# A hybrid-attention layer on one core: row copies moved from engines to DMA, weights loaded one step sooner, two head-stage steps issued later

## The chip, the core and the metric

The kernel runs on one core of a Trainium2 chip. The metric is the device time of one execution in microseconds (us). Of the program of before, three timed executions are shown, and one execution was profiled.

## What is computed

One layer on x of 1024 rows (the sequence) by 1024 columns, in float32 accuracy:

- h = RMSNorm(x) and P = h @ W_in. P's columns are split between two kinds of attention, which run beside each other.
- **mla**: 8 heads with compressed queries and keys, 96 numbers per head (64 plain, 32 rotated), 64 values, a block-causal mask over chunks of 64 rows, softmax.
- **ca**: 8 heads of 64 numbers; each chunk of 64 rows attends to itself and the 8 chunks before it, with a learned bias per head that depends on the clipped distance, softmax.
- x += concat(RMSNorm(mla), RMSNorm(ca)) @ W_out, and x += W_down(silu(g) * u), where [g|u] is a causal convolution of width 3 over RMSNorm(x) @ W_up.

## The kernel before, in words

TensorE (PE) multiplies in float32r, so every operand is held as a high and a low part and a product takes three matmuls (`mm3`, lines 136 to 139). The program order of every engine's queue is written out by hand; the tile framework adds only the waits (for data, and for a buffer that is to be used again). An instruction that waits holds up all that stands behind it in its own queue, and that goes for SyncE's queue (SP) of DMA issues and for GpSimd's (POOL) too.

The stages, by the span of the profiled execution: the latent projection (to about 75 us), 32 steps of the projection for the ca heads (to about 230), 16 heads (231 to 510), the output projection (to about 620), and the feed-forward layer.

**The 32 steps** (loop at line 818). Step i multiplies with one block of weights: `load_wc` (523) issues its DMA on SP, two steps ahead (819, 820); `split_wc` (547) makes its high part on ScalarE (ACT, 552) and its low part on VectorE (DVE, 553) one step ahead. Stages, weights and their parts all take buffers of one ring of ten (`p2`, 111), of which two more are taken for good at step 22 by `new_bias`. From step 22 on, `run_slot` puts the preparation of heads 0 and 1 between the matmuls.

**Preparation of a head** (`prep`, 652): a list of small jobs with a due time m. For head n from 2 on, m counts steps of the head stage from two heads earlier; for the first two heads it is mapped to the slots of the 32 steps. The jobs: `tr` transposes q and k on PE; `q_hi`, `k_hi` write their high parts (ACT, 674 and 682) and `q_lo`, `k_lo` the low ones (DVE, 678 and 688) into the operand set of the head (QH, K1, K2, QL, 1024 columns each; three sets in turn). A ca head has only 64 rows, so high and low parts are stacked: `dup_q` (690) and `dup_k` (696) copy 64 rows of 4 KB each, by DMAs that POOL issues; `zero` (693) clears 32 rows of QL on POOL. `bias_load` (711) fetches the bias table on SP. `mx` (732) computes the scores' maxima for the softmax on PE in 11 jobs, for ca with all 128 stacked rows, which DVE reduces in `mx_post` (739: lines 745, 749, 750); `mmax`, `mr` (756) and `mr_post` (758) turn the maxima into one row, which a DMA issued by POOL (760) puts into QL. Mask rows: `set_rows` (609) writes rows 96 to 112 of K2 and QL on ACT with two instructions (612), once for each of the three sets; `zero_rows` (605) clears 32 rows of K2 (607), on POOL for set 0 and on DVE for set 2, the latter at step 4 of the head stage (`ZERO_AT`, 962).

**The head stage** (loop at line 1110): 12 steps per head, even heads ca, odd heads mla. Step s computes scores of one tile (`score`, 901: matmuls 908 to 922, exponentials on ACT, 927 to 935); a step later `split` (938) makes the low part of the exponentials (948 to 950), on DVE for the steps of a head that `PLO_V` names, else on POOL; three steps later `pv` (953) multiplies with the values (958 to 960). After a head's last tile `finish` (1007) stores the 1024 sums by DMA (1011), and at step +3 `rec` (1013) inverts them, stores them to DRAM (1016) and loads them back spread over 64 rows (1017); ten and eleven steps later `mul` (1019) scales the output. For each pair of heads `o_sq` (967) squares on ACT (978) and adds to the running sums of squares on DVE, for one pair on POOL (979).

## Time and profile before

| | us |
|---|---|
| median of 3 timed executions | 1270.3 |
| lowest, highest of them | 1268.56, 1270.39 |
| the profiled execution's own time | 1271.62 |
| its span, first to last instruction | 1269.9 |
| PE busy | 1221.0 |
| DVE busy | 940.8 |
| POOL busy | 704.6 |
| ACT busy | 648.8 |

How to read it: the span is what the rows of the trace add up to; the profiled execution's own time is 1.72 us longer, and 1.3 us above the median. Busy times are sums over the span, and matmuls overlap one another in part. A row of the timeline names the start, the length, the engine, the source line, the operation, output and inputs, and in brackets the time that the engine stood idle before it and what ended that.

### The profile page before, as it was taken

What the parts mean: (1) busy time and instruction counts of PE and PEld (TensorE: products, weight loads), DVE (VectorE), ACT (ScalarE), POOL (GpSimd) and SP (SyncE); (2) the same over time, 40 slices, a digit from 0 to 9 for tenths busy, and PEclk for the clock granted to TensorE, in tenths of its full rate; (3) what the DMA queues carried; (4) which work ended last, traced back from release to release, by engine and by line L of the source; (5) the groups of instructions that cost most, each with busy time, mean ns of one, the idle gap of its engine ahead of it and who ended that gap; (6) DMA issues with size and microseconds to landing.
All of it is one profiled execution on the core that took longest, in us unless ns stands there. A gap on an engine that the chain in (4) does not pass through costs nothing.

```text
span 1269.9 us, 17774 instructions
## 1 busy us (share of the span) xinstructions
PE 1221.0 (96%) x5888; PEld 1004.7 (79%) x5888; DVE 940.8 (74%) x1623; ACT 648.8 (51%) x1338; POOL 704.6 (55%) x710
## 2 busy tenths in 40 slices
PE   9999998899998998999889999999999999999998
PEld 9888876787786876788668888888888888878887
DVE  6678565688888895466898766767776677888983
ACT  7562254678877887405555434334334344434442
POOL 4689750466564668204488767667677640425630
PEclk9999998999999999999999999999999999999999
DMA  9111213111111221265413332333322256933153
GB/s 353 36 35 50 59 56 78 26 44 43 27 37 37 43 64 52 100 232 174 141 59 121 120 99 84 108 108 105 119 81 86 91 181 243 363 92 116 59 197 127
DMA packets 102637, 134.78 MB, mean 106 GB/s; under 512 B 12152, under 2 KB 60816, under 8 KB 102544
## 3 DMA queue, kind: packets, MB, share of 16 engines
q1 hardware_dynamic: 100752, 129.37, 31.3%
q0 software_dynamic: 1792, 4.26, 1.7%
q8 instruction: 47, 0.77, 0.3%
q14 instruction: 46, 0.38, 0.1%
HBM read 97.47 MB, written 31.81 MB: 102 GB/s over the span
## 4 chain that ended last, share of the span: by engine, by line
PE 50%; DVE 8%; issue 2%; ACT 1%; POOL 1%; DVEq 0%; POOLq 0%; ACTq 0%
PE pb L139 11%; PE pb L138 11%; PE pb L137 11%; PE ps L137 6%; PE ps L139 5%; PE ps L138 5%; DVE ps L1438 1%; DVE as L1422 1%; DVE hq L1242 1%; POOL plo L950 1%; DVE wop L1359 1%; DVE h L1206 0%; DVE as L1421 0%; DVE as L1423 0%; DVE as L1424 0%
## 5 line engine op out<-in xcount | busy, mean ns | idle before, releaser
L950 POOL TENSOR_TENSOR plo<-misc,phi 128x512 fp32r<-128x512 f32 (+3 forms) x116 | 119.1, 1029 | 58.0 <-ACT phi L935 42.7
L1383 ACT ACTIVATE u<-ps,cols 128x1024 f32<-128x1024 f32 x44 | 53.2, 1208 | 178.0 <-DVE ps L1438 178.0
L137 PE MATMUL ps<-hq,wop 128*128 128x512 f32 x344 | 135.0, 393 | 2.6 <-ACT wop L1354 1.5
L139 PE MATMUL ps<-hq,wop 128*128 128x512 f32 x344 | 134.2, 390 | 1.8 <-DVE wop L1359 1.8
L138 PE MATMUL ps<-hq,wop 128*128 128x512 f32 x344 | 134.0, 390 | 0.2 <-DVE hq L1242 0.2
L138 PE MATMUL pb<-wring,aring 128*128 128x512 f32 x308 | 120.7, 392 | 2.1 <-DVE wring L1613 2.1
L137 PE MATMUL pb<-wring,aring 128*128 128x512 f32 x308 | 120.6, 391 | 0.3 <-DVE x2b L1438 0.3
L139 PE MATMUL pb<-wring,aring 128*128 128x512 f32 x308 | 120.6, 391 | 0.0
L1359 POOL TENSOR_TENSOR wop<-S,wop 128x512 fp32r<-128x512 f32 x42 | 63.3, 1507 | 96.4 <-ACT wop L1354 96.4
L137 PE MATMUL pb<-hq,wop 128*128 128x512 f32 x264 | 103.0, 390 | 2.3 <-ACT wop L1354 2.2
L139 PE MATMUL pb<-hq,wop 128*128 128x512 f32 x264 | 103.1, 390 | 0.2 <-DVE wop L1359 0.2
L138 PE MATMUL pb<-hq,wop 128*128 128x512 f32 x264 | 102.7, 389 | 0.0
L1610 DVE TENSOR_TENSOR aring<-ast,aring 128x512 fp32r<-128x512 f32 x77 | 71.1, 924 | 37.6 <-ACT aring L1609 37.6
L1609 ACT ACTIVATE aring<-ast 128x512 fp32r<-128x512 f32 x77 | 48.5, 630 | 93.7 <-PE pb L138 74.0
L932 ACT ACTIVATE misc<-pb 128x512 f32<-128x512 f32 (+3 forms) x116 | 56.3, 485 | 47.9 <-PE pb L918 20.0
L137 PEld LDWEIGHTS ps<-hq,wop 128*128 128x128 f32 x344 | 64.5, 188 | 20.0 <-DVE ps L1438 4.9
L138 PE MATMUL pb<-wl,hTh 128*128 128x512 f32 x192 | 75.8, 395 | 2.0 <-DVE wl L553 1.9
L139 PEld LDWEIGHTS ps<-hq,wop 128*128 128x128 f32 x344 | 64.6, 188 | 16.0 <-DVE wop L1359 2.5
L137 PE MATMUL pb<-wh,hTh 128*128 128x512 f32 x192 | 76.2, 397 | 0.0
L139 PE MATMUL pb<-wh,hTl 128*128 128x512 f32 x192 | 75.6, 394 | 0.0
L138 PEld LDWEIGHTS ps<-hq,wop 128*128 128x128 f32 x344 | 64.6, 188 | 13.7 <-DVE hq L1242 0.6
L204 POOL TENSOR_TENSOR stat<-stat,mhalf 128x1 f32<-128x1 f32 (+2 forms) x50 | 72.7, 1454 | 4.2
(331 smaller groups left out, 3629.8 us busy)
## 6 DMA issues: line engine op xcount, KB each, us to landing
wstage<-in_w_up_dram SPq DMA_DIRECT2D x43, 512.0 KB, 4.2
ast<-act_scratch SPq DMA_DIRECT2D x77, 256.0 KB, 4.5
act_scratch<-as SPq DMA_DIRECT2D x44, 256.0 KB, 2.3
wd<-in_w_down_dram SPq DMA_DIRECT2D x44, 256.0 KB, 5.5
act_scratch<-u SPq DMA_DIRECT2D x33, 256.0 KB, 2.1
x<-in_x_dram SPq DMA_DIRECT2D x16, 512.0 KB, 7.2
ws<-in_w_in_dram SPq DMA_DIRECT2D x32, 256.0 KB, 2.6
x_scratch<-x SPq DMA_DIRECT2D x14, 512.0 KB, 3.0
```

The lines of the kernel that those rows point to most:

```text
L137: T.matmul(o, lh, rh, start=start, stop=False)
L138: T.matmul(o, lh, rl, start=False, stop=False)
L139: T.matmul(o, ll, rh, start=False, stop=stop)
L204: G.tensor_tensor(dst, dst, mhalf[:, :n], op=ALU.pow)
L932: A.activation(p32[:, w], o[:, w], AF.Exp, scale=sc_)
L950: e.tensor_tensor(plo[:, w], p32[:, w], f(phi[:, w]), op=ALU.subtract)
L1242: lo_eng.tensor_tensor(lo, s3[:, ks], f(hi), op=ALU.subtract)
L1359: (V if n in W_LO_V or (j, n) in W0_LO_V else G).tensor_tensor(lo, s, f(hi), op=ALU.subtract)
L1383: A.activation(u, U, AF.Identity, scale=convw(2, c), bias=convb(c))
L1422: V.tensor_tensor(s[1], s[0], A11, op=ALU.subtract)
L1609: A.activation(ah, s, AF.Copy)
L1610: V.tensor_tensor(al, s, f(ah), op=ALU.subtract)
```

## The change

- `set_rows` writes the mask rows once, for set 0, on POOL instead of ACT, at slot 9; `copy_rows` copies them, for ca together with the zeroed rows of K2, to sets 1 and 2 by DMAs on SP. `zero_rows` clears its rows for set 0 alone, on POOL, and stores a block of zeros to DRAM; `zero` then loads QL's 32 rows of zeros from there (not for head 0, where `zero_rows` has cleared them).
- `dup_q`, `dup_k` and the DMA of `mr_post` are issued by SP instead of POOL.
- `mx` of head 0 uses the 64 rows of the high parts alone, and not the stacked 128.
- From step 20 of the 32 on, weights are loaded three steps ahead.
- In mla heads `PLO_V` no longer names step 6, so POOL makes that low part.
- `o_sq`'s additions for the second and third pair come three steps later than the squares; `spread`, the load of the inverted sums, comes two steps after `rec` (heads 0 to 13).

```diff
--- before.py
+++ after.py
@@ -31,8 +31,9 @@
 PI_IN = 3.1415925
 PHI_M = 24
 PHI_0 = 18
-PLO_V = (1, 3, 6, 8, 10)
+PLO_V = (1, 3, 6, 8, 10), (1, 3, 8, 10)
 LAG = 3
+WC_AHEAD = 20
 MR = 18
 MX_CA = 9
 STORE = 2
@@ -49,7 +50,6 @@
 OSQ_G = ("mla", 2),
 SIDE_AT = 3
 SIDE_2 = 5, 6, 8
-ZERO_AT = 4
 WARM = 18
 END_PLO_V = range(180, 192, 2)
 
@@ -554,6 +554,7 @@
             wsp[i] = wh, wlo
 
     dsc = nc.dram_tensor("bias_scratch", (2, 8, 384), F32, kind="Internal").ap()
+    dzero = nc.dram_tensor("zero_scratch", (32, 1024), F32, kind="Internal").ap()
     dden = nc.dram_tensor("den_scratch", (16, 1024), F32, kind="Internal").ap()
     mcols = [const([128, 24], F32, f"mcol{i}") for i in range(2)]
     mrow = const([8, 128], F32R, "mrow")
@@ -602,15 +603,24 @@
         st = sets[i]
         st.QH, st.K1, st.K2, st.QL = [b[:, 1024 * i:1024 * i + 1024] for i in range(4)]
 
-    def zero_rows(i):
-        if heads[i][0] == "ca":
-            (V if i == 2 else G).memset(f(sets[i].K2[64:96]), 0.0)
-
-    def set_rows(i):
-        st = sets[i]
+    def zero_rows():
+
+        st = sets[0]
+        G.memset(f(st.K2[64:96]), 0.0)
+        G.memset(f(st.QL[64:96]), 0.0)
+        nc.sync.dma_start(dzero, f(st.QL[64:96]))
+
+    def set_rows():
+        st = sets[0]
         for dst, c in ((st.K2, 0), (st.QL, 16)):
-            A.activation(dst[96:113].rearrange("p (t i) -> p t i", t=16),
-                         mk[96:113, c:c + 16, None].to_broadcast([17, 16, 64]), AF.Copy)
+            G.tensor_copy(dst[96:113].rearrange("p (t i) -> p t i", t=16),
+                          mk[96:113, c:c + 16, None].to_broadcast([17, 16, 64]))
+
+    def copy_rows(i):
+
+        r = 64 if heads[i][0] == "ca" else 96
+        nc.sync.dma_start(f(sets[i].K2[r:113]), f(sets[0].K2[r:113]))
+        nc.sync.dma_start(f(sets[i].QL[97:113]), f(sets[0].QL[97:113]))
 
     def new_v(i):
         b = sv(F32R, "vset")
@@ -688,13 +698,13 @@
             V.tensor_tensor(o, p[0:d], f(st.K2[0:d, c]), op=ALU.subtract)
 
         def dup_q():
-            G.dma_start(st.QH[64:128], st.QH[0:64])
+            nc.sync.dma_start(f(st.QH[64:128]), f(st.QH[0:64]))
 
         def zero():
-            G.memset(f(st.QL[64:96]), 0.0)
+            nc.sync.dma_start(f(st.QL[64:96]), dzero)
 
         def dup_k():
-            G.dma_start(st.K1[0:64], st.K2[0:64])
+            nc.sync.dma_start(f(st.K1[0:64]), f(st.K2[0:64]))
 
         def v_post():
             if n < 2:
@@ -733,7 +743,7 @@
             p = hold["m", j] = bank()
             for t, part, k_, w, off in jobs()[j]:
                 w = max(w, 256)
-                q_, k2 = (st.QH, st.K1) if is_ca else (st.QH[0:d], st.K2[0:d])
+                q_, k2 = (st.QH, st.K1) if is_ca and n else (st.QH[0:d], st.K2[0:d])
                 T.matmul(p[:, off:off + w], q_[:, t * 128:t * 128 + 128], k2[:, k_:k_ + w], start=True, stop=True)
 
         def mx_post(j):
@@ -757,7 +767,7 @@
 
         def mr_post():
             V.tensor_scalar(mrow, hold.pop(("m", 10))[0:8, 0:128], -1.0, None, op0=ALU.mult)
-            G.dma_start(st.QL[96:97].rearrange("p (t s) -> p t s", t=8), mrow)
+            nc.sync.dma_start(f(st.QL[96:97]).rearrange("p (t s) -> p t s", t=8), f(mrow))
 
         r = [(1, "pe", lambda: tr(0, 0)), (2, "pe", lambda: tr(0, 1)), (3, "pe", lambda: tr(1, 0)),
              (4, "pe", lambda: tr(1, 1)),
@@ -765,7 +775,9 @@
              (4, "post", lambda: k_hi(0)), (4, "post", lambda: q_lo(1)),
              (5, "post", lambda: k_hi(1)), (5, "post", lambda: k_lo(0)), (6, "post", lambda: k_lo(1))]
         if is_ca:
-            r += [(1, "post", zero), (4, "post", dup_q), (5, "post", dup_k), (-1, "post", lambda: bias_load(0)), (6, "post", bias_nat),
+            if n:
+                r += [(1, "post", zero)]
+            r += [(4, "post", dup_q), (5, "post", dup_k), (-1, "post", lambda: bias_load(0)), (6, "post", bias_nat),
                   (6, "post", lambda: bias_load(1)), (14, "post", bias_tr)]
         for j in range(11):
             m = min((MX_CA if is_ca else 6) + max(j - 1, 0), 17)
@@ -816,8 +828,10 @@
                 fn()
 
     for i, (c, k, ts) in enumerate(steps):
-        if i + 2 < len(steps):
+        if i == WC_AHEAD:
             load_wc(i + 2)
+        if i + 2 + (i >= WC_AHEAD) < len(steps):
+            load_wc(i + 2 + (i >= WC_AHEAD))
         if i < 4:
             rope_tables(i)
         if i == 3:
@@ -847,12 +861,12 @@
                         first.setdefault((b, ph), []).append(fn)
                     else:
                         micro.setdefault((first_slot(n, m, ph), n, m, PH.index(ph)), []).append(fn)
-            micro[16, 9, 0, 0] = [lambda: set_rows(0)]
-            micro[26, 9, 0, 0] = [lambda: set_rows(1)]
+            micro[9, 9, 0, 0] = [set_rows]
+            micro[20, 9, 0, 0] = [lambda: copy_rows(1)]
         if i == 24:
             for n in range(2):
                 new_set(n)
-                zero_rows(n)
+            zero_rows()
         for t in ts:
             if i >= 22:
                 run_slot(slot)
@@ -889,14 +903,14 @@
     OB = [misc[:, 1024 * i:1024 * i + 1024] for i in range(2)]
     bias_tab(misc[:, 2048:2944])
     new_set(2)
-    set_rows(2)
+    copy_rows(2)
     opair, O, wo, sqs = {}, {}, {}, {}
 
     turn = [0]
 
     def plo_v(s, n):
 
-        return s % 12 in PLO_V if n < 14 else s in END_PLO_V
+        return s % 12 in PLO_V[n % 2] if n < 14 else s in END_PLO_V
 
     def score(s, n, i, pc_):
         kind, h = heads[n]
@@ -959,24 +973,32 @@
         T.matmul(o[0:64], vs.VL[:, kt, :], phi[:, 0:n], start=False, stop=False)
         T.matmul(o[0:66], vs.VH[:, kt, :], plo[:, 0:n], start=False, stop=stop)
 
-    later = {ZERO_AT: [lambda: zero_rows(2)]}
+    later = {}
 
     def at(s, fn):
         later.setdefault(s, []).append(fn)
 
-    def o_sq(kind, j, c):
+    def o_sq(kind, j, c, s0):
+
         w = slice(c, c + 512)
         o = opair[kind, j][:, w]
         if j == 0:
             if c == 0:
                 sqs[kind] = blk(F32, "sqs")
             A.activation(sqs[kind][:, w], o, AF.Square)
+            return
+        if c == 0:
+            opair["sq"] = blk(F32, "sq")
+        sq = opair["sq"][:, w]
+        A.activation(sq, o, AF.Square)
+
+        def add():
+            (G if (kind, j) in OSQ_G else V).tensor_tensor(sqs[kind][:, w], sqs[kind][:, w], sq, op=ALU.add)
+
+        if j < 3:
+            at(s0 + 3, add)
         else:
-            if c == 0:
-                opair["sq"] = blk(F32, "sq")
-            sq = opair["sq"][:, w]
-            A.activation(sq, o, AF.Square)
-            (G if (kind, j) in OSQ_G else V).tensor_tensor(sqs[kind][:, w], sqs[kind][:, w], sq, op=ALU.add)
+            add()
 
     def o_part(kind, j, c):
 
@@ -1012,9 +1034,10 @@
 
         def rec():
             V.reciprocal(d8, d8)
-            row = dden[n]
-            nc.sync.dma_start(row.rearrange("(p c) -> p c", c=8), d8)
-            nc.sync.dma_start(R[64:128], dap(row, 0, [[0, 64], [1, 1024]]))
+            nc.sync.dma_start(dden[n].rearrange("(p c) -> p c", c=8), d8)
+
+        def spread():
+            nc.sync.dma_start(R[64:128], dap(dden[n], 0, [[0, 64], [1, 1024]]))
 
         def mul(c):
             if (kind, h // 2) not in opair:
@@ -1024,13 +1047,14 @@
                             op=ALU.mult)
 
         at(s + 3, rec)
+        at(s + (5 if n < 14 else 3), spread)
         s0 = s + (11 if n < 14 else 9)
         at(s0 - 1, lambda: mul(0))
         at(s0, lambda: mul(512))
         if h % 2:
             j = h // 2
-            at(s0 + 2, lambda: o_sq(kind, j, 0))
-            at(s0 + 4, lambda: o_sq(kind, j, 512))
+            at(s0 + 2, lambda: o_sq(kind, j, 0, s0 + 2))
+            at(s0 + 4, lambda: o_sq(kind, j, 512, s0 + 4))
             if kind == "ca":
                 s0 = max(s0, O_CA[j])
             at(s0, lambda: o_part(kind, j, 0))
```

## Rows read from the trace of the kernel before

**Rows 1.** Stretches: length; busy PE, PEld, DVE, ACT, POOL; clock; DMA share; GB/s.
```profile
199.00:231.00 32.00, 25.32 (x110) 19.73 (x109) 17.94 (x54) 12.07 (x22) 0.65 (x2) 0.89 0.18 43
231.00:491.00 260.00, 244.19 (x1488) 198.02 (x1487) 218.12 (x582) 205.73 (x507) 161.23 (x209) 1.00 0.18 43
```
**Rows 2.** Timeline, 195 to 216 us: the end of the 32 steps.
```profile
195.95 0.59 ACT L682 ACTIVATE set<-pb 64x512 fp32r<-64x512 f32 x1
...
202.97 1.08 PE L737 MATMUL pb<-set 128*128 128x256 f32 x3 [3.61 <-DMA set<-set]
203.39 0.72 ACT L552 ACTIVATE wh<-ws,gmix 128x512 fp32r<-128x512 f32 x1 [5.92 <-DMA ws<-in_w_in_dram]
...
212.07 2.00 ACT L612 ACTIVATE set<-mk 17x1024 fp32r<-17x1024 f32 x2
...
214.59 0.42 DVE L720 TENSOR_TENSOR bl<-tb,bh 128x256 fp32r<-128x256 f32 x1 [2.61 <-issue]
```
**Rows 3.** Busy time in two stretches at the lower clock, columns as in rows 1.
```profile
203.00:208.80 5.80, 5.80 (x16) 4.70 (x17) 2.86 (x10) 0.72 (x1) 0.00 (x0) 0.50 0.19 55
495.50:498.90 3.40, 3.29 (x11) 2.57 (x11) 1.58 (x3) 2.93 (x8) 3.14 (x7) 0.50 0.02 1
```
**Rows 4.** What PE waited for, 199 to 232 us: total us, times, longest.
```profile
PE pb L737 <- DVE mcol L745: 2.5, 2, 1.6
```
**Rows 5.** What PE waited for in the heads, 231 to 491 us.
```profile
PE pb L960 <- POOL plo L950: 6.5, 10, 1.1
PE pb L756 <- DVE mcol L753: 2.2, 3, 0.9
PE pb L958 <- DVE phi L948: 1.5, 2, 0.8
PE pb L737 <- DMA set<-set: 1.0, 1, 1.0
PE pb L958 <- DVE mcol L745: 1.0, 1, 1.0
...
PE pb L958 <- issue: 0.5, 1, 0.5
```
**Rows 6.** Timeline of the preparation of head 4, 276 to 281 us.
```profile
276.31 0.58 ACT L682 ACTIVATE set<-pb 64x512 fp32r<-64x512 f32 x1
...
277.19 0.56 POOL L697 DMA_DIRECT2D set<-set  x1 [1.05 <-ACT phi L927]
...
277.77 1.28 POOL L950 TENSOR_TENSOR plo<-misc,phi 128x512 fp32r<-128x512 f32 x1
...
279.10 0.45 PE L960 MATMUL pb<-plo,vset 128*66 128x512 f32 x1 [1.07 <-POOL plo L950]
...
280.35 0.44 PE L737 MATMUL pb<-set 128*128 128x256 f32 x2
```
**Rows 7.** DMA issues: KB each, median us to landing.
```profile
ws<-in_w_in_dram SPq DMA_DIRECT2D x32, 256.0 KB, 2.6
...
set<-set POOLq DMA_DIRECT2D x16, 256.0 KB, 3.0
misc<-den_scratch SPq DMA_DIRECT2D x16, 256.0 KB, 3.5
```
**Rows 8.** Landing of the eight copies that line 697 issues.
```profile
DMA to landing us min/median/max: 2.9/3.1/6.0
```
**Rows 9.** Timeline of DVE, 379 to 385 us: the additions of one pair.
```profile
379.01 0.69 DVE L979 TENSOR_TENSOR sqs<-sqs,sq 128x512 f32<-128x512 f32 x1 [1.18 <-ACT sq L978]
...
382.44 2.15 DVE L979 TENSOR_TENSOR sqs<-sqs,sq 128x512 f32<-128x512 f32 x1
```
**Rows 10.** Groups by shape: busy us, mean ns of one, idle before and its releasers.
```profile
L950 POOL TENSOR_TENSOR plo<-misc,phi 128x512 fp32r<-128x512 f32 x54 | 71.8, 1329 | 49.3 <-ACT phi L935 36.6 <-PE pb L922 10.3 <-PE pb L960 2.2
...
L950 DVE TENSOR_TENSOR plo<-pb,phi 128x512 fp32r<-128x512 f32 x18 | 12.3, 682 | 7.5 <-ACT pb L928 7.5
...
L694 POOL MEMSET set<- 32x1024 f32 x8 | 7.6, 946 | 0.4
```

## The prediction, made before the changed kernel was run

> **What bounds the kernel now.** I read the busy times by stretch first. PE is the bound: of the 260 us of the heads it works 244.2, of the 32 us before them 25.3 [rows 1]. So nothing is won but PE's idle time, 6.7 us ahead of the heads and 15.8 in them, and what a low clock costs. Next come the timeline, the clock, and PE's waits.
>
> Ahead of the heads PE stands 3.61 us until the copies of head 0's set have landed, though the rows that were to be copied were written by 196.54 (195.95 + 0.59) [rows 2]. After that idle time the granted clock is 0.50, the 1.2 GHz level, for the 5.8 us from 203.0, in which PE is busy throughout [rows 3]; at 2.4 GHz that work takes half, so 2.9 us are lost. Later ACT writes mask rows for 2.00 us and DVE stands still for 2.61 us behind it [rows 2]; the maxima come late and PE waits 1.6 us for a bank that they hold, and 0.9 more at another place [rows 4].
>
> In the heads the largest wait of PE is for POOL's low parts: ten times, 6.5 us in all [rows 5]. One by one these are four of about 1.04 (4.1 together), one of 0.7 at the first tile, and five small ones (1.7). The timeline of head 4 shows how the large ones arise: POOL waits in its queue to issue `dup_k` until ACT has written the keys (276.31 + 0.58 = 276.89), issues at 277.19, and makes the low part from 277.77; PE gets it 1.07 us late. But the first `mx`, at 280.35, needs that same copy, which can land at 277.19 + 3.1 = 280.29 at the earliest [rows 6, 8]. The gap hides a wait that stands right behind it.
>
> **The change part by part**, against the profiled execution (1271.62 us; span 1269.90, 1.72 around it; the median 1270.3 is 1.3 lower).
>
> *Stage before the heads, 7.6 us.* Head 0's `mx` no longer reads the copied rows, so the 3.6 goes, and the 2.9 of low clock with it, if PE finds no other reason to stand. The next late thing would be weights: ACT got the block of step 28 only at 203.39 after 5.92 us of idling [rows 2], since its load stood on SP behind the bias load. Three steps ahead it is issued one step sooner, in front of `dup_k` and that bias load. It is covered; without this edit I count 0 to 1 us. The extra buffer comes out of the ring of ten; a load then waits for older matmuls to end, which lie two steps back. `set_rows` leaves ACT: 1.6 gone. On POOL its two copies have no row; for 1024 columns between a memset of 32x1024, 0.95, and two subtractions of 512 columns, 2.66 [rows 10], so 1.9 to 5.3 us, nearer the former, since they have one input. POOL works 0.65 us in this stretch [rows 1], so they cost nothing; without that cover the copies to sets 1 and 2 would land later, before heads that start much later. What is late next is DVE: 17.9 us of work in what would be 24 [rows 1]. I give back 0.5 for that and leave its other waits, 1.4 (0.9 for `mcol` and 0.6 of another), in place: 3.6 + 2.9 + 1.6 - 0.5 = 7.6. Ends: 9.6 if all 6.7 and the 2.9 go, 4.0 if DVE takes 3.6 us more.
>
> *Start of the heads, 1.2.* `set_rows` for set 2 holds ACT for a like 2.00 us as the first exponentials are due; the 0.5 of line 958 and the 0.7 of line 960 [rows 5] go. Bounds 0.5 and 1.2. The copy on SP that replaces it serves head 2, 24 steps later.
>
> *Head 2, 1.5.* DVE's `zero_rows` leaves (a like memset on POOL is 0.95 [rows 10]), and with it 0.9 before line 756; the 1.0 wait for `dup_k` [rows 5] shrinks, I take 0.6 of it. Bounds 0.5 and 1.9.
>
> *Copies on SP, heads 4, 6, 8 and 12, 2.1.* POOL loses a memset (0.95), two issues like the 0.56 [rows 6, 10] and the row of `mr` per ca head, so the gap of about 1.04 goes. What remains is `mx` behind `dup_k`. In head 4 it starts 280.35 - 276.89 = 3.46 after the keys [rows 6]. On SP no 0.30 passes between keys and issue, I take 0.03; how long SP's queue needs for 64 rows of 4 KB from SBUF to SBUF no row shows. Bounds: 2.6, its loads of the same size in 128 rows, and 3.5, 64 rows of the same length from DRAM; POOL's own copies 3.0 [rows 7]. I take 2.8, between the first and the last of these, because the source is SBUF. With 0.1 to the start PE waits until 2.93 and gains 0.53 a head, 2.1 in four. At 2.6 it is 2.9, without any wait 4.1, at 3.5 a loss of 0.7. SP itself gets four more issues per ca head and one per mla head, each under its neighbours' 0.5 us, in a queue that is mostly waiting. Those that wait there are `zero` (for the set's last reader), `dup_q` and `dup_k` (ACT) and `mr` (DVE). Ahead of `dup_k` stand only `dup_q` and the store of the sums, both earlier work; behind it the bias table, due eight steps later.
>
> The Trainium skill speaks against a better landing (DMA: Bandwidth & Descriptors, "Issuing engines are not separate DMA queues"): DMAs of all issuers run on the same 16 engines, so another issuer saves only issue time. By it the landing stays as POOL's row has it, and this term becomes 1.1.
>
> *Additions later, heads 10 and 14, 3.5.* DVE now waits 1.18 for ACT's square and then takes 0.69 or even 2.15 per addition [rows 9]. The maxima and a cleared tile come late: 1.3 of line 756's 2.2, the 1.5 of line 958 and 1.3 of small waits of line 960 [rows 5], 4.1. Three steps later the square is done and the place in the queue is not a critical one; 0.6 goes back to the wait for `dup_k`. Bounds 1.8 and 4.1.
>
> The Trainium skill (SBUF — State Buffer, "Who interferes with whom") says that a DVE instruction with two SBUF inputs is blocked by a POOL instruction that reads SBUF; the 2.15 beside a POOL low part bears it out. The late additions again stand in steps with a POOL low part. By that rule they would block again; it is a rival below.
>
> *mla heads, 0.5.* Step 6's low part takes POOL 1.33 us instead of DVE 0.68 [rows 10], seven times, beside 161 busy of 260 [rows 1]. The 1.0 of line 958 [rows 5], a bank held by a late DVE, goes. In head 13 POOL also has output weights and additions to do and is full; there I lose 0.5. Bounds -1.1 and 2.
>
> *`spread`* costs nothing: at +5 instead of +3 with 260/191 = 1.36 us a step its 3.5 us landing [rows 7] ends 3.3 us before `mul` at +10; without that slack DVE would wait there. SP is freed of a wait.
>
> After 491 nothing changes; the low clock at 495.5 [rows 3] stays.
>
> Sum: 7.6 + 1.2 + 1.5 + 2.1 + 3.5 + 0.5 = 16.4. 1271.6 - 16.4 = 1255.2, less 1.3: **1254 us**.
>
> **The rivals.**
> - *The gap only moves.* `dup_k` lands after 3.5 us, 4.2 in head 2. For it speaks how close `mx` stands behind the copy in head 4 [rows 6]; against it SP's 2.6 [rows 7]. Copies -0.7, additions 2.2, head 2 0.3: 11.1 gained, 1259.
> - *Additions still block.* 1.7 of the 3.5 and 0.8 of the mla heads stay: 13.9 gained, 1256.
> - *DVE takes over before the heads* as PE speeds up: 4.0 there instead of 7.6, 1257. For it: two waits for DVE are there already [rows 4].
> - *Head 0's `mx` still waits*, because the framework sees the whole set as one buffer. Against it: low keys were written to K1's upper half while the lower half's copy was under way, so it tells them apart. Then 6.5 stays: 1260.
> - *Slower: SP's queue delays the copies.* Zeros, queries, keys and the bias table follow one another there. The longest landing of a `dup_k`, among other transfers, was 6.0 [rows 8]. At 6.0 the first `mx` comes 2.67 later than now in four heads, 1.5 in head 2 and 1.4 each in two: 15 lost against 9.6 gained elsewhere. Four such waits with a stretch like the second one of rows 3 behind each (3.29 busy at half rate, 1.6) make 6.6 more: 1282. It decides from 5.2 us of landing on; the medians of 2.6 to 3.5 [rows 7] speak against it.
>
> **How the numbers follow.** A measurement of this kernel tells 0.2%, 2.5 us, from no change. Forecast 0.5; gap moves 0.16; additions block 0.12; DVE takes over 0.1; `mx` still waits 0.05; slower 0.04; 0.03 for gains that come back elsewhere, no change. So faster 0.92, which I lower to 0.91, same 0.04, slower 0.05. Range: all terms at their best ends (9.6 + 1.2 + 1.9 + 4.1 + 4.1 + 2 = 22.9) give 1247, and 1245 if the second low-clock stretch goes too; two rivals at once (stage before the heads 4.0, gap moves) are 7.5 gained, 1263. That holds the listed cases but the last two: 1245 to 1263.
>
> **What would show it.** Right: no wait of PE for set copies before the heads and no low clock at 203; line 612 gone from ACT; PE's wait for line 950 below 3 us in the heads, and line 737 waiting for a set's copy some 0.2 to 0.6 us per ca head. Wrong: line 737's waits above 1 us each, a second step waiting for weights, or DVE as PE's releaser for over 4 us between 199 and the heads' start.

## The result, and the profile after

| | before | after |
|---|---|---|
| median, us (4 executions each) | 1270.35 | 1259.09 |
| ratio, with its 95% interval | | 0.9891 (0.9874 to 0.9909) |
| profiled execution | 1271.62 | 1259.34 |
| its span | 1269.9 | 1257.6 |
| median of the second comparison | 1271.17 | 1257.07 |
| its ratio | | 0.9891 (0.9875 to 0.9908) |

Of the changed kernel's four executions one took 3114.98 us, a slow one that no profile explains; it is in the median above and not in the ratio, and without it the median is 1258.84. The ratio on record is not the quotient of the two medians, which is 0.991.

The kernel became 1.1% faster, 11 to 14 us. The forecast of 1254 rests on a gain of 16.4 us against the profiled execution of before. To see where the two part, I cut the spans at three waits of PE that every trace has: for the split weights (`wl`, 0.7 us), for DVE in the maxima ahead of the heads (about 0.55), and for POOL near the end of the heads (2.06). The timeline of PE in the changed kernel has them here; a row begins with the start of the matmul behind the wait, and the bracket holds the wait.

```profile
192.52 0.50 PE L138 MATMUL pb<-wl,hTh 128*128 128x512 f32 x1 [0.73 <-DVE wl L553]
...
220.74 0.41 PE L747 MATMUL pb<-set 96*128 96x384 f32 x1 [0.54 <-DVE pb L759]
...
481.96 0.33 PE L972 MATMUL pb<-phi,vset 128*66 128x256 f32 x1 [2.06 <-POOL phi L962]
```

The first profile of before has them at 189.31, 223.04 and 493.68. The lengths between them, in us, follow for all kernels of this text; the kernel before and the changed one were each profiled twice:

| kernel | to the first mark | end of the 32 steps | heads | rest |
|---|---|---|---|---|
| before, first profile | 189.3 | 33.73 | 270.64 | 776.2 |
| before, second | 191.4 | 33.68 | 269.96 | 778.8 |
| after, first | 192.5 | 28.22 | 261.22 | 775.6 |
| after, second | 190.3 | 28.29 | 261.29 | 776.2 |
| all ca maxima from 64 rows | 192.3 | 28.23 | 272.60 | 775.4 |
| head 0's from 96 rows | 191.3 | 25.85 | 261.24 | 775.9 |
| head 0's from 128 rows | 191.1 | 26.88 | 262.00 | 775.6 |
| key copy in two halves | 190.3 | 28.30 | 258.01 | 776.4 |
| copies issued by POOL | 191.7 | 28.24 | 263.74 | 776.4 |
| mask and zero rows by engines | 192.7 | 29.29 | 263.86 | 777.4 |
| additions at once | 192.4 | 28.26 | 265.56 | 776.8 |
| step 6 on DVE | 188.5 | 28.30 | 261.44 | 776.0 |
| weights and spread as before | 191.1 | 27.96 | 267.30 | 776.2 |
| three edits together | 191.5 | 25.82 | 256.93 | 778.1 |

The two middle columns hold what the change touches, and in the two kernels that were profiled twice they agree to 0.1 us from one execution to the next (0.7 for the heads of before). The outer columns hold next to nothing that it touches (ahead of the first mark the earlier weight loads) and vary by 3 to 4 us. So a part of the change is read far better from the middle columns than from the total; but each variant has one profile, and differences of a few tenths prove nothing. By the means of the two profiles, the change gained 33.70 - 28.26 = 5.4 us at the end of the 32 steps and 270.30 - 261.26 = 9.0 in the heads: **14.5 us, against 16.4 foretold**.

The outer part explains why the two first profiles differ by only 12.3: the first one of after lost 3.2 us ahead of the first mark. The stretches of the changed kernel, with the columns of [rows 1], show it, and the stages:

```profile
202.35:228.90 26.55, 25.25 (x111) 17.52 (x111) 18.18 (x55) 8.28 (x18) 0.00 (x0) 1.00 0.14 41
228.90:479.40 250.50, 242.58 (x1488) 198.79 (x1487) 209.25 (x570) 202.31 (x506) 149.15 (x182) 1.00 0.20 49
50.00:56.50 6.50, 6.13 (x19) 5.47 (x20) 4.86 (x20) 0.49 (x1) 3.39 (x12) 0.51 0.00 0
202.50:210.00 7.50, 7.50 (x33) 4.76 (x33) 3.81 (x14) 2.13 (x4) 0.00 (x0) 1.00 0.47 140
```

From 50 to 56.5 us the granted clock was 0.51, near the 1.2 GHz level, behind a wait of PE of 2.86 us that was 1.40 in the first profile of before; nothing of the change lies there. PE's idle time ahead of the heads went from 6.7 [rows 1] to 26.55 - 25.25 = 1.3 us, in the heads from 15.8 to 7.9, and the stretch at 203 that ran at half clock [rows 3] now runs at 2.4 GHz. What is left, by the same view as [rows 4] (195 to 232 us) and [rows 5] (228.9 to 479.4 us), in the changed kernel:

```profile
PE pb L747 <- DVE pb L759: 0.5, 1, 0.5
PE pb L747 <- DVE mcol L755: 0.5, 1, 0.5
PE pb L747 <- DVE set L688: 0.3, 1, 0.3
...
PE pb L747 <- DMA set<-set: 4.2, 7, 0.8
PE pb L974 <- POOL plo L964: 2.0, 3, 1.1
PE pb L681 <- DVE plo L964: 0.8, 1, 0.8
```

The wait for POOL's low parts fell from 6.5 us to 2.0, those for the row of maxima behind DVE (line 756 of before) are gone, and in their place the first maxima (line 747) wait for the key copy in seven ca heads, 4.2 us in all. In head 4 the timelines of ACT, SP and PE give this chain in the changed kernel, the answer to [rows 6]:

```profile
270.69 0.59 ACT L692 ACTIVATE set<-pb 64x512 fp32r<-64x512 f32 x1
...
271.30 0.48 SPq L707 DMA_DIRECT2D set<-set  x1
...
274.44 0.65 PE L747 MATMUL pb<-set 128*128 128x256 f32 x3 [0.76 <-DMA set<-set]
```

Keys written at 271.28, the copy issued 0.02 later, the maxima start 3.16 after the keys, where it was 3.46. The list of DMA issues gives the median landing, the answer to [rows 7]; it did not become shorter than POOL's 3.0:

```profile
set<-set SPq DMA_DIRECT2D x16, 256.0 KB, 3.1
```

### The profile page after: what moved, and what is told of

It reads as the page before. It is cut to its first block, busy times and chain, and to the rows that moved or that the text cites. A ratio compares the mean times of both kernels' runs of the same rounds, so it can differ in the third digit from the quotient of the medians.

```text
span 1257.6 us, 17771 instructions
## 1 busy us (share of the span) xinstructions
PE 1220.4 (97%) x5888; PEld 1004.8 (80%) x5888; DVE 934.5 (74%) x1615; ACT 641.4 (51%) x1332; POOL 692.2 (55%) x680
## 4 chain that ended last, share of the span: by engine, by line
PE 49%; DVE 7%; POOL 2%; issue 2%; ACT 1%; DMA 0%; SPq 0%; POOLq 0%; DVEq 0%; ACTq 0%
PE pb L139 10%; PE pb L137 10%; PE pb L138 10%; PE ps L137 6%; PE ps L139 5%; PE ps L138 5%; DVE as L1446 1%; DVE ps L1462 1%; POOL plo L964 1%; DVE x2b L1462 1%; DVE as L1445 0%; DMA ast<-act_scratch 0%; POOL hq L1266 0%; DVE as L1447 0%; DVE as L1448 0%
## 5 line engine op out<-in xcount | busy, mean ns | idle before, releaser
L964 POOL TENSOR_TENSOR plo<-misc,phi 128x512 fp32r<-128x512 f32 (+3 forms) x123 | 128.0, 1043 | 78.9 <-ACT phi L949 54.6
L946 ACT ACTIVATE misc<-pb 128x512 f32<-128x512 f32 (+3 forms) x123 | 60.7, 493 | 43.2 <-PE pb L936 18.7
```

The source lines that it names most:

```text
L946: A.activation(p32[:, w], o[:, w], AF.Exp, scale=sc_)
L964: e.tensor_tensor(plo[:, w], p32[:, w], f(phi[:, w]), op=ALU.subtract)
```

## The experiments

All start from the changed kernel; medians are in us, the ratio is against the kernel before, and lengths are those of the table.

**All ca maxima from 64 rows.** In the changed kernel head 0's maxima alone use 64 rows, and its trace has holes around them.

```diff
-                q_, k2 = (st.QH, st.K1) if is_ca and n else (st.QH[0:d], st.K2[0:d])
+                q_, k2 = (st.QH[0:d], st.K2[0:d])
```

> The changed kernel with the maxima of all eight ca heads taken from 64 rows (head 0 alone does so in the changed kernel); the maxima then come from the high parts alone and do not wait for the copy of the keys. Theory A (a matmul with 64 rows among such with 128, or beside them, costs PE about 0.1 us before it and 0.2 after it; head 0 lost 2.6 us so, by the start-to-start times in the trace of the changed kernel): seven more heads at 2.6 are +18.2, less the 4.2 us of waits for copies that go: +14 against the changed kernel, about 1273 us, and the same holes of 0.33 ahead of and 0.3 to 0.4 behind each line of maxima in the heads. Theory B (the holes in head 0 are waits on semaphores or data in that busy stage, and 64 rows cost nothing): only the waits go, -4.2, about 1255 us.

Median 1271.27, ratio 0.9993 (0.9981 to 1.0006): the whole gain is gone. The heads last 272.60 instead of 261.26, 11.3 more. In 228.9 to 490.6 us of this kernel, the same stretch, PE is busy almost throughout, at a granted clock of 1.00, and its timeline in head 4 shows the price on both sides of a maximum:

```profile
228.90:490.60 261.70, 259.73 (x1487) 197.69 (x1486) 213.80 (x569) 203.02 (x506) 146.01 (x182) 1.00 0.19 47
```

```profile
278.60 0.34 PE L974 MATMUL pb<-plo,vset 128*66 128x384 f32 x1
278.87 0.43 PE L747 MATMUL pb<-set 64*128 64x384 f32 x1
279.23 0.50 PE L934 MATMUL pb<-set 96*128 96x512 f32 x1
```

Start to start it is 0.27 us from a matmul of 384 columns to the maximum, and 0.36 from there to the next, where two others of 384 columns stand 0.17 to 0.18 apart. That is 0.1 ahead and 0.2 behind, with no wait in brackets and at that clock. The waits for the copy are gone, so seven heads pay 11.3 + 4.2 = 15.5 us, 2.2 each: theory A, with 2.2 for the 2.6 expected. Theory B falls.

**Head 0's maxima from 96 rows.** The 32 rows that are added multiply zeros.

```diff
-                q_, k2 = (st.QH, st.K1) if is_ca and n else (st.QH[0:d], st.K2[0:d])
+                m = 96 if n == 0 else d
+                q_, k2 = (st.QH, st.K1) if is_ca and n else (st.QH[0:m], st.K2[0:m])
```

> The changed kernel with head 0's maxima taken from 96 rows instead of 64 (rows 64 to 95 of the keys are the zeroed ones, so the result is the same; the queries' rows are those that the copy of the queries has filled). Theory A (only 64 rows cost, 96 rows do not, as the mla heads' maxima show with 0.23 us start to start): -2.5 against the changed kernel in the stage before the heads, about 1256.5 us, unless PE now waits for the copy of the queries, issued at 198.2 and landed after 3.0, 1.4 us before the first maximum. Theory B (the holes are waits): no difference, 1259.

Median 1257.36, ratio 0.9890 (0.9871 to 0.9908), which by itself tells nothing; the end of the 32 steps is 25.85 instead of 28.26, **2.4 us less**, and nothing else moved. One of the maxima, in the timeline of PE of the changed kernel and then of this one:

```profile
205.68 0.40 PE L139 MATMUL pb<-wh,hTl 128*128 128x512 f32 x1
206.00 0.44 PE L747 MATMUL pb<-set 64*128 64x384 f32 x1
206.37 0.64 PE L681 MATMUL pb<-identr,nqk 128*96 128x128 f32 x4
```

```profile
205.86 0.39 PE L139 MATMUL pb<-wh,hTl 128*128 128x512 f32 x1
206.09 0.34 PE L748 MATMUL pb<-set 96*128 96x384 f32 x1
206.27 0.60 PE L681 MATMUL pb<-identr,nqk 128*96 128x128 f32 x4
```

With 64 rows 0.32 and 0.37 us pass from start to start, with 96 rows 0.23 and 0.18. The Trainium skill (TensorEngine Tiling (Array Packing), "Key Properties") says that a change of tiling mode, of which 64 rows by 128 columns is one, drains TensorE; the holes around matmuls of 64 rows among such of 96 and more fit that, at 0.3 us for going there and back. That a plain matmul of 64 rows enters that mode is argued from the fit, not shown. Since 96 rows of the same operands have no holes, the operands are not the cause.

**Head 0's maxima from 128 rows,** as before the change.

```diff
-                q_, k2 = (st.QH, st.K1) if is_ca and n else (st.QH[0:d], st.K2[0:d])
+                q_, k2 = (st.QH, st.K1) if is_ca else (st.QH[0:d], st.K2[0:d])
```

> The changed kernel with head 0's maxima taken from all 128 stacked rows again, as before the change. The prediction's view (the cut is what removes the 3.6 us wait and the 2.9 of low clock): both come back, +6.5 less the 2.6 that the 64 rows cost, about 1263 us. Rival (the copy of the keys, issued by SP at 199.8 without the bias load ahead of it, lands near 202.9 and the first maximum stands at 202.6): PE waits 0.3 to 1 us, no low clock, and the 2.6 of the 64 rows go: -1.6 to -2.3, about 1257 us.

Median 1257.50, ratio 0.9892 (0.9872 to 0.9911); the end of the 32 steps is 26.88, 1.4 us shorter than in the changed kernel, and the rival is right. The timelines of SP and PE of this kernel:

```profile
198.32 0.47 SPq L707 DMA_DIRECT2D set<-set  x1
198.89 0.52 SPq L722 DMA_DIRECT2D tb<-bias_scratch  x1
...
201.97 0.65 PE L747 MATMUL pb<-set 128*128 128x256 f32 x3 [0.86 <-DVE wl L553]
```

The copy is issued ahead of the bias load, and PE starts 3.65 us later, so it landed in at most that; POOL's took 6.0 [rows 8], with the bias load issued by SP at the same time; which of the transfers beside it made it late is not shown. (The `wl` named had been done for 0.9 us; the copy is the other input.) Of the 3.61 us wait 0.86 is left, and the clock stays up. In the heads 0.7 is lost here: the waits for key copies are 5.0 us instead of 4.2. No edit explains it.

**The key copy in two halves.** Each half follows its half of the keys; the first maxima read the first half alone.

```diff
-        def dup_k():
-            nc.sync.dma_start(f(st.K1[0:64]), f(st.K2[0:64]))
+        def dup_k(i):
+            c = slice(i * 512, i * 512 + 512)
+            nc.sync.dma_start(f(st.K1[0:64, c]), f(st.K2[0:64, c]))
...
-            r += [(4, "post", dup_q), (5, "post", dup_k), (-1, "post", lambda: bias_load(0)), (6, "post", bias_nat),
+            r += [(4, "post", dup_q), (4, "post", lambda: dup_k(0)), (5, "post", lambda: dup_k(1)), (-1, "post", lambda: bias_load(0)), (6, "post", bias_nat),
```

> The changed kernel with the copy of the keys made by two DMAs of 512 columns each, the first one right behind the first half of the keys' high part, one step (about 1.4 us) earlier. The first maxima read the first half alone. Theory A (the waits of 0.4 to 0.8 us in the seven ca heads after the first are for the landing of 3.1 us and nothing stands right behind them): the waits go, 4.2 us in all, about 1255 us. Theory B (the wait moves again, to the second half, to ACT or to DVE): less than 1.5 us are gained, about 1258.

Median 1255.12, ratio 0.9871 (0.9850 to 0.9892); the heads last 258.01, 3.3 us less. Of what PE waited for in this kernel's heads (228 to 480 us), what lies behind DVE's low parts and maxima:

```profile
PE pb L681 <- DVE plo L965: 1.6, 2, 1.0
PE pb L935 <- DVE mcol L756: 0.8, 3, 0.3
PE pb L748 <- DVE mcol L756: 0.3, 1, 0.3
```

In the whole list no wait for a set's copy is left. Of the 4.2 us, 1.4 came back behind DVE, whose low parts now stop PE for 1.6 us (0.8 in the changed kernel) and whose maxima for 1.1 (0.5); PE's busy time, on the other side, is 0.7 less. Theory A, less a fifth.

**Copies and row issued by POOL.**

```diff
-            nc.sync.dma_start(f(st.QH[64:128]), f(st.QH[0:64]))
+            G.dma_start(f(st.QH[64:128]), f(st.QH[0:64]))
...
-            nc.sync.dma_start(f(st.K1[0:64]), f(st.K2[0:64]))
+            G.dma_start(f(st.K1[0:64]), f(st.K2[0:64]))
...
-            nc.sync.dma_start(f(st.QL[96:97]).rearrange("p (t s) -> p t s", t=8), f(mrow))
+            G.dma_start(f(st.QL[96:97]).rearrange("p (t s) -> p t s", t=8), f(mrow))
```

> The changed kernel with the copies of queries and keys and the row of maxima issued by POOL again. The landing takes 3.1 us from either queue, so by theory A the copy's issuer is worth only what POOL's queue loses to it: the copy is issued 0.3 later, POOL's low part stands 0.6 behind it, and PE's wait of about 1 us for that low part returns in heads 4, 6, 8 and 12 with the wait for the copy after it gone or small: +0.3 a head, about +1.4, 1260.5 us. Rival (the prediction's full term with SP's landing at 2.8 or better): +2 to +4, 1261 to 1263. Rival (another issuer changes nothing, since all issuers share the same engines): within 0.5.

Median 1261.09, ratio 0.9923 (0.9909 to 0.9936); the heads last 263.74, 2.5 us more, and the end of the 32 steps is unchanged. The timeline of PE in this kernel, at heads 4 and 6:

```profile
273.01 0.45 PE L974 MATMUL pb<-plo,vset 128*66 128x512 f32 x1 [1.07 <-POOL plo L964]
...
307.49 0.45 PE L974 MATMUL pb<-plo,vset 128*66 128x512 f32 x1 [0.93 <-POOL plo L964]
```

The waits at heads 8 and 12 are 1.07 each, too. These four are those of before, 4.1 us again, where in the changed kernel PE waits 0.76, 0.47, 0.71 and 0.75 for the copy, 2.7. So **the four heads gained 1.4 by the new issuer**, as theory A has it. What theory A left out is the other three ca heads: there waits of 0.83, 0.93 and 0.94 for POOL stand where the changed kernel waits 0.57, 0.43 and 0.50 for the copy, another 1.2. With them the 2.5 falls into the rival's +2 to +4, but not for the rival's reason: the landing is no shorter from SP. That all issuers are alike falls, and so does the full 2.1 of the forecast in those four. The eight key copies that POOL issues here land as they did before the change [rows 8]; the 6.0 is head 0's:

```profile
DMA to landing us min/median/max: 2.9/3.0/6.0
```

**Mask and zero rows by engines,** with none of the new DMAs of rows; the old `set_rows`, `zero_rows` and `zero` at their old places.

```diff
-            micro[9, 9, 0, 0] = [set_rows]
-            micro[20, 9, 0, 0] = [lambda: copy_rows(1)]
+            micro[16, 9, 0, 0] = [lambda: set_rows(0)]
+            micro[26, 9, 0, 0] = [lambda: set_rows(1)]
...
-    copy_rows(2)
+    set_rows(2)
...
-    later = {}
+    later = {4: [lambda: zero_rows(2)]}
```

> The changed kernel with the mask rows written by ACT for each of the three sets, and the zero rows by POOL and DVE, as before the change (no copies of rows by DMA). Theory A (the prediction's terms for them: 1.6 before the heads, 0.5 to 1.2 at their start, 0.9 in head 2): +3.0 to +3.7, about 1262.5 us, with DVE's stall of about 2.6 us behind ACT near 212 back. Rival (with the wait for the copies gone, PE is no longer close behind ACT there, so the writes are covered): +1 or less.

Median 1263.61, ratio 0.9941 (0.9929 to 0.9954). The two stages are 1.0 and 2.6 us longer, 3.6 together: theory A. The places are those of the forecast: ACT writes for 2.00 us as the first exponentials are due, and PE waits for the row of maxima behind DVE's clearing of zero rows, as in [rows 5], line 756, but for 1.8 us instead of 0.9: behind the clearing DVE's combination of the maxima (`mmax`) takes 1.13 us beside a low part on POOL, where it took 0.22 before the change. DVE's stall behind ACT near 212 is 1.3 us, half of what was expected. ACT, DVE and PE in the timeline of this kernel:

```profile
230.40 2.00 ACT L613 ACTIVATE set<-mk 17x1024 fp32r<-17x1024 f32 x2
...
239.95 1.13 DVE L760 TENSOR_TENSOR mcol<-mcol 128x8 f32<-128x8 f32 x1
...
241.14 0.27 PE L763 MATMUL pb<-identr,mcol 128*8 128x128 f32 x1 [1.79 <-DVE mcol L760]
```

**Additions at once.**

```diff
-        if j < 3:
+        if j < 0:
```

> The changed kernel with the additions of the sums of squares right behind the squares again, as before the change. Theory A (the prediction's: the late addition costs the heads with a pair's end 3.5 us in all): +3.3, about 1262 us, with waits of 0.3 to 0.8 us of PE for DVE's maxima and low parts back in heads 10 and 14. Rival (the later additions block as well, or POOL's lighter load took the waits away by itself): +1.7 or less, about 1260.

Median 1263.54, ratio 0.9945 (0.9931 to 0.9959); the heads last 265.56, 4.3 us more, above theory A's 3.3. What PE waited for in the heads of this kernel:

```profile
PE pb L766 <- DVE mcol L763: 3.5, 2, 1.7
```

Both large waits, 1.75 us each, stand where a pair of heads ends, near 374 and 446 us, for the row of maxima. POOL and DVE in the timeline of this kernel at the first of them:

```profile
374.31 1.26 POOL L964 TENSOR_TENSOR plo<-misc,phi 128x512 fp32r<-128x512 f32 x1 [0.21 <-ACT phi L949]
374.34 1.25 DVE L763 TENSOR_TENSOR mcol<-mcol 128x8 f32<-128x8 f32 x1
```

The additions, at most 0.95 us here, do not take the 2.15 of [rows 9] again. It is `mmax` that comes late, behind an addition and DVE's 1.18 us of waiting for ACT's square, and then takes 1.25 us beside POOL's low part; in the changed kernel it comes ahead of that low part and takes 0.15. So the 4.3 us are the worth of the later additions in the changed kernel; they are not the same waits as those of before that the forecast added up. And the late additions do not block, by the group of line 996 in the changed kernel (six of its ten additions are the late ones), 682 ns each with 0.2 us of idling ahead of them, beside 1008 ns and 3.7 before:

```profile
L996 DVE TENSOR_TENSOR sqs<-sqs,sq 128x512 f32<-128x512 f32 x10 | 6.7, 682 | 0.2 <-ACT sq L993 0.2
```

**Step 6 on DVE again.**

```diff
-PLO_V = (1, 3, 6, 8, 10), (1, 3, 8, 10)
+PLO_V = (1, 3, 6, 8, 10), (1, 3, 6, 8, 10)
```

> The changed kernel with step 6's low part of the mla heads on DVE again. Theory A (the trace: heads 11 and 9 gained about 1.9 by it, head 13 lost 1.9): no difference over 1 us, with waits for DVE of 0.5 to 1.0 us back in head 11 and waits for POOL in head 13 gone. Rival (the prediction's upper end: 2.0 gained): +2, about 1261.

Median 1258.64, ratio 0.9902 (0.9885 to 0.9920); the heads last 261.44, 0.2 more, within what two executions can differ by. The gain of the earlier mla heads and the loss in head 13 cancel, as theory A said: from the second mark to the first maxima of the last ca head this kernel takes 227.8 us and the changed one 226.4, and ahead of the third mark 1.2 of these 1.4 come back, with the waits of 0.7 and 1.1 for POOL gone. The waits for DVE that were expected in head 11 are not in its trace.

**Weights and spread as before.** The two edits that the prediction costs at nothing.

```diff
-WC_AHEAD = 20
+WC_AHEAD = 99
...
-        at(s + (5 if n < 14 else 3), spread)
+        at(s + 3, spread)
```

> The changed kernel with weights two steps ahead throughout, and the spread of the inverted sums right behind their store, as before the change: the two edits that the prediction costs at nothing. Theory A (covered): within 1 us of the changed kernel, 1258 to 1260. Rival (the weights of step 28 are late as PE no longer waits, and SP's queue, blocked by the spread's wait, holds up the copies): +1 to +3, with waits of PE for the split weights between 199 and 205 us or longer waits for copies in the heads.

Median 1263.99, ratio 0.9950 (0.9936 to 0.9964): **the heads last 267.30, 6.0 us more**, and the end of the 32 steps 0.3 less. Theory A falls, and the rival is right in its second half, but for another transfer than it named, and for more than its +1 to +3. SP's timeline in head 4, in the changed kernel's second profile and then in this one:

```profile
269.68 0.58 SPq L1037 DMA_DIRECT2D den_scratch<-den  x1
270.38 0.57 SPq L722 DMA_DIRECT2D misc<-bias_scratch  x1
271.09 0.71 SPq L770 DMA_DIRECT2D set<-mrow  x1
272.32 0.48 SPq L1040 DMA_DIRECT2D misc<-den_scratch  x1
```

```profile
270.54 0.58 SPq L1037 DMA_DIRECT2D den_scratch<-den  x1
273.18 0.46 SPq L1040 DMA_DIRECT2D misc<-den_scratch  x1
273.75 0.52 SPq L722 DMA_DIRECT2D misc<-bias_scratch  x1
274.32 0.70 SPq L770 DMA_DIRECT2D set<-mrow  x1
```

The spread (line 1040) waits on SP until the store ahead of it has landed, 2.6 us after that was issued. Behind it in the same queue stand the bias load and the row of maxima (line 770), which is now issued 3.8 us after the store instead of 1.4. PE's next mla score needs that row. What PE waited for in this kernel (226 to 495 us) has a line that the changed kernel doesn't have:

```profile
PE pb L936 <- DMA set<-mrow: 4.1, 7, 0.8
```

Not all of the 6.0 is the spread's. Behind a wait of 1.07 us for POOL, which the changed kernel has as well, ten matmuls run at half clock in this execution, and the same ten at full clock in the second one of the changed kernel (busy times as in [rows 1], from the end of the wait on, in this kernel and in that):

```profile
473.17:476.60 3.43, 3.43 (x10) 2.64 (x11) 1.21 (x3) 0.45 (x2) 2.92 (x5) 0.51 0.00 0
```

```profile
468.29:470.20 1.91, 1.91 (x10) 1.55 (x11) 1.09 (x2) 0.45 (x2) 1.91 (x2) 1.00 0.00 1
```

That is 1.5 us, and as such stretches come and go from one execution to the next (see below), **about 4.5 us** are left for the spread, 0.4 of them a longer wait for head 2's key copy.

**The changed kernel once more.**

> The changed kernel once more, on the same chip as the three that follow, as their base. If the stretch at half clock from 50 to 56 us of its first profile (about 3 us lost, in a stage that the change does not touch) belongs to some executions only, the time may come out up to 3 us lower than 1259; if it belongs to the program, 1259 again and the same stretch in the profile.

Median 1257.07, ratio 0.9891 (0.9875 to 0.9908): 2 us lower than the first time at the same ratio. **The kernel before once more**, for its profile:

> The kernel before, once more, for its profile alone: does a stretch at half clock follow the gap at 48 us here too? If the change has nothing to do with it, some executions of the kernel before have it; its length in the executions of the changed kernel and its variants so far is 3 to 6 us, none in the first profile of the kernel before.

This execution took 1275.47 us. The same stretch from 50 to 56.5 us, in the second profile of before and the kernel with step 6 on DVE:

```profile
50.00:56.50 6.50, 5.90 (x25) 5.20 (x26) 4.91 (x21) 1.12 (x4) 3.49 (x13) 0.74 0.00 0
```

```profile
50.00:56.50 6.50, 6.50 (x37) 5.92 (x36) 4.79 (x19) 3.21 (x15) 2.64 (x11) 1.00 0.00 0
```

Granted clocks of 0.74 and 1.00, of 0.78 in the second profile of after and 0.51 in its first: it belongs to executions and not to the change, and the first profile of before was one without it. Where it is missing, the first mark comes at 188.5 to 189.3, else at 190.3 to 192.7.

**Three edits together:** head 0's maxima from 96 rows, the key copy in two halves, and

```diff
-        return s % 12 in PLO_V[n % 2] if n < 14 else s in END_PLO_V
+        return s % 12 in PLO_V[n % 2 if n < 13 else 0] if n < 14 else s in END_PLO_V
```

> The changed kernel with three edits: head 0's maxima from 96 rows, the copy of the keys in two halves, and the low part of step 6 on DVE again in head 13 alone, where POOL is full. Theory A (the gains add up, since each lies on PE's own path): -2.5, -4 and about -2.5 (waits of 0.7, 1.1 and 2.1 us for POOL at 467 to 482 in the changed kernel get shorter by one low part, 1.28 us), about 1250 us. Theory B (PE's waits move on to DVE and POOL as it speeds up): half of it, about 1254.

Median 1254.02, ratio 0.9868 (0.9852 to 0.9883), the lowest median here, 3.1 below the changed kernel beside it, though the intervals of the two still overlap; theory B by the total. By the stages it is 2.4 and 4.3 us shorter, 6.8 together, three quarters of theory A's 9, but its profile gives back 1.9 behind the heads. What PE waited for behind DVE's low parts in its heads (228 to 480 us):

```profile
PE pb L681 <- DVE plo L966: 1.6, 2, 1.0
```

The wait of 2.06 us for POOL at the end of the heads is untouched. In this execution a stretch at the lower clock follows it, in the second one of the changed kernel none does (4 us from about the mark on, in this kernel and in that):

```profile
474.00:478.00 4.00, 3.47 (x12) 2.55 (x13) 2.27 (x4) 3.00 (x8) 3.98 (x9) 0.62 0.00 0
```

```profile
480.00:484.00 4.00, 3.58 (x18) 2.23 (x19) 2.19 (x5) 3.16 (x8) 3.99 (x7) 1.00 0.00 0
```

That is not why the total gained less than the stages: the kernel with the key copy in two halves has the stretch as well (0.60 in the 4 us behind its mark), and its rest is 776.4; the second profile of before has none (1.00), and its rest is 778.8. What gave back the 1.9 stays open.

## Why the prediction was right, and where its steps failed

The direction, the bound (PE, and only its idle time and its clock) and the range held. The sum of 16.4 met 14.5 in the stages: 7.6 met 5.4 ahead of the heads, the other 8.8 met 9.0, with errors that partly cancel and one that the sum doesn't show. That the 9.0 come so near the 8.8 is in part luck.

- *Stage before the heads, 7.6 foretold, 5.4 measured.* The waits fell by 5.4 (6.7 to 1.3; the step had 3.6 + 1.6 - 0.5 = 4.7), and the 2.9 of low clock came in full. The step that failed is "Head 0's `mx` no longer reads the copied rows", taken as a gain only: 64 rows cost PE 2.4 us there (2.8 of busy time, 0.4 of which takes the place of a wait for DVE that is back with 96 rows). No row of before had a matmul of 64 rows, and the term should have had a bound for it.
- *Why the wait went.* The same step gave the 3.6 and the 2.9 to the cut of `mx`. With 128 rows PE waits 0.86 and keeps its clock; with the cut but POOL as the issuer it waits for no copy either, though that copy again lands only after 6.0. So, with the rest of the change in place, either edit removes most of the wait, and without the cut this stage is 1.4 us shorter.
- *Mask and zero rows.* The terms were 1.6, 1.2 and 0.9, 3.7; undone, they cost 1.0 and 2.6, 3.6, of which 0.9 is the slow `mmax` beside POOL that the forecast did not have. POOL's two copies took 1.04 and 1.17 us, 2.2, near the lower bound that was preferred, and nothing waited for them.
- *Copies on SP, 2.1 foretold, 1.4 measured in the four heads.* The mechanism was right, the landing mis-sized: 2.8 taken, "because the source is SBUF", 3.1 measured, as from POOL. The Trainium skill's rule (DMA: Bandwidth & Descriptors, "Issuing engines are not separate DMA queues") gave 1.1 there, and the trace agrees with it in these heads: only the issue time is saved. (By the prediction's own formula a landing of 3.0 gives 1.3 and one of 3.1 gives 0.9.) The rival that the gap only moves is true for two thirds of it (2.7 of 4.1). The wait for head 2's copy went from 1.05 to 0.57, 0.5 of the 0.6 taken.
- *Additions later, 3.5 foretold, 4.3 measured by undoing them.* The step "the maxima come late" holds. The rival by which the additions block again falls: 682 ns each. But much of what comes back when they are undone is `mmax` beside POOL's low part, a wait that the forecast's list doesn't have; that the two numbers are near each other is partly luck.
- *mla heads, 0.5 foretold, 0.2 measured,* no more than two executions can differ by, with the loss in head 13 that was named: both parts were larger than taken, 1.4 won and 1.2 lost instead of 1.0 and 0.5.
- *Weights three steps ahead, costed at nothing:* so it is, within what one profile can tell; without it the stage is 0.3 shorter.
- *"`spread` costs nothing".* Nothing here speaks against that for the term by itself, ahead of `mul`; it was not run without the issue edit. But with `mr`'s row on SP its delay is worth about 4.5 us: left at its old place it would have held that row behind its own wait in SP's queue. I listed `mr` among what SP issues, and checked who stands ahead of `dup_k`, but not who stands behind `spread`. The sum does not show this, because the change makes both edits; a forecast of the issue edit alone would probably have been far too good, since the 2.5 that this edit is worth beside the later spread are less than the 4.5. That pair was not run.
- *Rivals.* DVE did not take over (1.3 us of waits ahead of the heads, the limit given was 4); the copies land 3.1 us after their issue by the list above, far from the 5.2 at which slower would decide; head 0's `mx` does not wait for the copy. Of the signs that were named one was missed: the waits of line 747 are 0.43 to 0.76 us per head and not 0.2 to 0.6. (The chances of the cases with a gain add up to 0.93, not 0.92.)
- *The rest.* Against the first profile the gain is 12.3, because that execution of before had no stretch at low clock near 50 us and that of after had, behind a wait that was 1.5 us longer. A sum made against one execution carries such a difference with it.

## What to carry to other kernels

When a DMA moves to another queue, walk that queue in order and look at each wait that now stands ahead of it; a step that is costed at nothing can be what makes the move pay. A narrower matmul among full ones is not free: look at the start-to-start times on both sides of it, since such holes bear no wait in the trace. And where a total varies by 3 us from one execution to the next, cut the span at waits that all traces share: the stages that the change touches repeated to 0.1 us here, but for 0.7 in the heads of before; then look at the granted clock in them, as 1.5 of the 6.0 us of one variant were a stretch at the lower clock.

## What the runs showed of the hardware that was not expected

- A matmul of 64 rows between ones of 96 to 128 rows costs 0.1 us ahead of it and 0.2 behind it at full clock; 96, 105 and 113 rows cost nothing there.
- The same wait of PE, 2.06 us near the end of the heads, is followed by some 4 us with a granted clock of 0.62 in one execution and of 1.00 in another, and a wait of 1.07 us ahead of it by 0.51 in one and 1.00 in another. Ahead of the stretch at 50 us the waits themselves differ, from 0.98 to 3.24 us; but 1.40 is followed there by 1.00 (first profile of before) and 1.41 by 0.74 (key copy in two halves). The time to the first mark differs by 2.1 us between the two profiles of the kernel before, and by 2.2 between those of the changed one.
- SBUF-to-SBUF copies of 64 rows of 4 KB land, in the median, 3.0 to 3.1 us after their issue from either queue; only head 0's took 6.0 from POOL, with other loads issued beside it, and at most 3.65 from SP.
- DVE's combination of two blocks of maxima (`mmax`, 128x8) takes 0.15 us at its shortest and, when it starts behind the start of a low part on POOL, 1.13 and 1.25 us, to about that low part's end.
